# Hybrid decoder trunk on one core: pool halo copies, value-weight splits, the boundary norms and the MLP's token norm reordered

## The chip, the cores and the metric

The kernel runs on one core of one Trainium2 chip. TensorE (PE) multiplies matrices, VectorE (DVE), ScalarE (ACT) and GpSimd (POOL) work on elements, and SyncE (SP) issues most of the transfers. The metric is the device time of one execution in microseconds; a kernel's time is the median of its runs. The profiled execution is one more run, with its own time.

## What is computed

A decoder layer with a final norm, in float32, for one sequence of 2048 tokens of width 1024: a mixer (retention heads beside a causal pooling mixer) with an output projection, cross-attention into 256 memory tokens, and a gated MLP with a short convolution. The parts that the change touches:

```python
def rmsnorm(x, g):
    x32 = x.astype(jnp.float32)
    y = x32 * lax.rsqrt(jnp.mean(x32 * x32, axis=-1, keepdims=True) + EPS)
    return (y * g.astype(jnp.float32)).astype(x.dtype)

def pool_mixer(u, w, scale):
    ...
    for gi, wlen in enumerate(POOL_WINDOWS):      # 2, 4, 8, 16
        ...
        mean = (c - lower) / count                # mean over the trailing window
        groups.append(mean - u32[:, :, gi * POOL_GROUP:(gi + 1) * POOL_GROUP])
    ...

def cross_attn(h, mem_n, wq, wkv, wo):
    ...
    s = jnp.einsum('bshd,bmhd->bhsm', q, k).astype(jnp.float32) * (XA_HEAD_DIM ** -0.5)
    p = jax.nn.softmax(s, axis=-1).astype(v.dtype)
    o = jnp.einsum('bhsm,bmhd->bshd', p, v).reshape(B, S, D_MODEL)
    return o @ wo

def reference(...):
    ...
        x = x + jnp.concatenate([y_ret, y_pool], axis=-1) @ w_out[l]
        x = x + cross_attn(rmsnorm(x, xa_norm_g[l]), mem_n, xa_wq[l], xa_wkv[l], xa_wo[l])
        x = x + conv_glu_ffn(rmsnorm(x, ffn_norm_g[l]), ffn_w_up[l], ffn_conv_w[l],
                             ffn_conv_b[l], ffn_w_down[l])
    return rmsnorm(x, final_norm_g)
```

## The kernel before

**Arithmetic.** Each float32 operand is split in two rounded parts, high and low, and each product is three matmuls (high by high, high by low, low by high: L241, L242, L243 in `passes`). A split is two instructions: ACT copies the high part (L233), and DVE subtracts it from the original (L216, the line of the helper `tt`, which records most additions, subtractions and products). In the profile R is a raw weight as it came by DMA, Q a pair of its parts, G the arena that holds split activations and the diagonals, T a temporary, Z a larger buffer, mm a PSUM accumulator of a matmul, and aux a PSUM tile for small work.

**Stages.** Tokens go in two blocks of 1024, each as two halves of 512 columns; channels lie on the 128 partitions. For each block: the values, the four retention heads and four pool groups (`pool_group`), the output projection, the attention (`attention`), and its value products (`unit` with the weights `VWd`, eight tiles of 128 x 1024, each one of 48 matmuls). Then comes the MLP of both blocks (`run`). The memory-side weight products come first, beside block 0. All through block 0 and 1, `weight_sums` is stepped as `under[0]`: it adds MLP weight blocks in memory, by SP transfers and by accumulating POOL transfers (L919).

**What sets the order.** The program is written as Python generators that are stepped inside `unit` (one step of `behind[0]` after each quarter of a unit's matmuls). The framework then orders the instructions of each engine by a simulated timeline, inserts the semaphore waits, and leaves each engine a fixed sequence: what stands behind a waiting instruction on its engine waits too. `tc.issue_after(ins)` around a piece of code orders that piece's instructions behind `ins` where they are on the same engine.

**Pool group.** The evacuation `evac` (L627) takes the matmul result into u with 16 columns of room ahead, copies the previous half's last 16 columns in (L630) and saves this half's last 16 (L631), both on POOL; then DVE forms the window sums by doubling (1 to 4 additions of 128 x 527 to 128 x 513) and the result is split for the next product.

**Norms.** `stats` (L308) sums squared activations over partitions with one-column matmuls (L315) and runs three Newton steps on DVE; `rows_norm` (L1410) copies the result into rn. `spread` (L323) turns the 128 x 8 table into a row per token on all partitions: it splits rn (yh, yl), and for each half of 512 tokens DVE builds two diagonals (L216, G<-consts,yh and G<-consts,sm), PE multiplies them by ones (L339) and ACT copies the sum (L344). At the block boundary the generator `norms` (L1594) does this as `behind[0]`: the next block's table, the own block's table (used in the MLP), the spread. The four value weights of block 1 are loaded and split there too (L657), and pool groups 3 and 2 run ahead of the values.

**Attention.** 16 score tiles, eight for each of two pairs of heads. Each: matmuls, row maximum, exponential on ACT (L875), reciprocal and scaling on DVE; `turn` (L847) transposes the tile two tiles later (L850) and splits the result. The softmax scale comes from the norm of the block, formed after the first tile. The loads of the first VWd tiles go out during the attention, and their splits stand wherever the simulated timeline puts them. In block 1 the attention is stepped together with `first_tiles`, which forms the MLP's normed inputs of block 0 from tiles of Xd, and writes them and their sums to Hd.

**Token norm in the MLP.** For block 1 the normed inputs are formed during the MLP: `later_tiles` loads four half tiles of Xd and steps `normed_tiles` by a due-time list, one step every two ticks (`after(2, step)`); its first step does all four products.

Of the kernel before, what the change touches and what calls it, by code (L numbers as in the profile page):

```python
# [2 lines left out]

# [12 lines left out]
P = 128  # L16
# [5 lines left out]
SUB = 512  # L22
# [97 lines left out]
def trunk(ctx, tc, xT, memT, pos, w_qkgu, w_v, wkv, wqT, wo, wout_r, wout_p, poolT, w_up, w_dn, vecs, consts, outT):  # L120
# [156 lines left out]

    quarter, slow = [0], [True]
    behind, under, fetched = [iter(())], [iter(())], [None]

    def finish():
        for _ in behind[0]:
# [2 lines left out]
    def unit(raw, rhs, evac, order=range(4)):  # L285


        hs = pairs(raw)
        ps = [mmps() for _ in range(NS)]
        for h in range(2):  # L290
            for s in range(NS):
                for j, kk in enumerate(order):
                    k = 4 * h + kk
                    w = [hs[h][:, i, kk * P : (kk + 1) * P] for i in range(2)]
                    passes(ps[s], w, rhs(k, s), h + j == 0, h == 1 and j == 3)
                next(behind[0], None)
# [26 lines left out]
    def spread(y, outs, keep=True, late=False):  # L323

        yh = smp.tile([P, 8], F32R, tag="yh", name=nm("yh"), bufs=1)[:, : y.shape[1]]
        yl = small(y.shape[1])
        dve.tensor_copy(yh, y)
        tt(dve, yl, y, yh.bitcast(F32), ALU.subtract)
        at = 0

        one_pair = prs.take() if late else None
        for out in outs:
            n = out.shape[1] // P
            d = one_pair if late else B.take()
            ps = aux()[:, : n * P]
            for i, v in enumerate((yh.bitcast(F32), yl)):
                di = d.r[:, i * SUB : i * SUB + n * P]
                last = tt(dve, di.rearrange("p (a b) -> p a b", a=n), ident.rearrange("p (o b) -> p o b", o=1).to_broadcast([P, n, P]), bcast(v[:, at : at + n], P), ALU.mult)
                pe.matmul(ps, ones, di, start=i == 0, stop=i == 1)  # L339
# [6 lines left out]
        return last  # L346

    def squares(k, src, s_ap, eng=dve):

# [274 lines left out]
    def pool_group(b, g, rb):  # L624
        out = B.take(2)

        def evac(s, ps):  # L627
            u, *bufs = [TT.take() for _ in range(3 if g else 2)]
            tt(dve, u.f[:, 16 : 16 + SUB], ps, rb[s].f[:, :SUB], ALU.mult)
            pool.tensor_copy(u.f[:, 0:16], phalo[:, g])  # L630
            pool.tensor_copy(phalo[:, g], u.f[:, SUB : SUB + 16])  # L631
            src, lo = u, 1
            for i in range(g + 1):
                sh = 1 << i
                dst = bufs[i % 2]
                tt(dve, dst.f[:, lo : 16 + SUB], src.f[:, lo : 16 + SUB], src.f[:, lo - sh : 16 + SUB - sh], ALU.add)
                src = dst
                lo += 2 * sh
            cur, d = u.f[:, 16 : 16 + SUB], src.f[:, 16 : 16 + SUB]
            w = 2 << g  # L640
            if b == 0 and s == 0:
                tt(dve, d[:, :w], d[:, :w], icnt[:, :w], ALU.mult)
# [179 lines left out]
    def attention(sums, beside, pace):  # L822
# [24 lines left out]
        def turn(pt, t, e):  # L847
            tp = aux()
            for j in range(4):
                pe.transpose(tp[:, j * P : (j + 1) * P], e.f[:, j * P : (j + 1) * P], ident)  # L850
            pt4 = pt.r.rearrange("p (i k t) -> p i k t", i=2, t=T)[:, :, :, t * P : (t + 1) * P]
            split(tp.rearrange("p (k t) -> p k t", k=4), pt4[:, 0], pt4[:, 1])
            e.free()

        mw = [[], []]
        for _ in load_m(0):
            pass
# [568 lines left out]
    def normed_tiles(b, j, q, rb):  # L1426

        for i, v in enumerate(q):
            n, s = j + 4 * (i // 2), i % 2
            stt(v, v, ffng[:, n : n + 1], rb[s].f[:, :SUB], ALU.mult, ALU.mult)  # L1430
        if j == KT // 2 - 1:
            for r in rb:
                r.free()
        yield
        send(Hd[b, j], {0: q[0], 5: q[3], 3: q[2]})
        t = TT.take()
        todo = sums_of(*q, t.f[:, :SUB])
# [27 lines left out]
    def later_tiles(b, j, rb):  # L1465

        x = fetch_tiles(b, j)
        steps = normed_tiles(b, j, [r.f[:, :SUB] for r in x], rb)

        def step():  # L1470
            if next(steps, True) is None:
                after(2, step)
            else:
                for r in x:
                    r.free()

        after(2, step)
# [18 lines left out]
    for b in range(NB):  # L1496
# [68 lines left out]
        for n in range(KT):  # L1565
            if n + 1 < KT:
                fetch_acc(n + 1)

            def rhs(k, s):
                at = (k % 4) * T + s * SUB  # L1570
                return tuple(prob[k // 4].r[:, i * 4 * T + at : i * 4 * T + at + SUB] for i in range(2))

            unit(load_tile(VWd[n]), rhs, add_residual(b, n, xs, acc=acc[n]))
            act.dma_start(Xd[b, n], acc[n].f)
            if b + 1 < NB:
                load_x(n, nxt, got)
# [12 lines left out]
        if b + 1 < NB:  # L1589
            normed, own = [None, [], None], []  # L1590
            for u in acc:
                u.free()

            def norms(xs, nxt, normed, own):  # L1594

                normed[0] = rows_norm(nxt)
                yield
                own.append(rows_norm(xs))
                yield
                normed[1] += [TT.take() for _ in range(NS)]  # L1600
                spread(normed[0], [r.f[:, :SUB] for r in normed[1]])
                yield

            behind[0] = norms(xs, nxt, normed, own)
# [119 lines left out]
```

## Time and profile before

| | |
|---|---|
| runs | 2498.81, 2500.07, 2504.08 us; median 2500.07 |
| profiled execution | 2497.77 us, its span 2496.0 us |
| instructions in the span | 33121 |
| mean granted TensorE clock | 0.993 |
| moved by DMA | 474.27 MB, mean 190 GB/s |

The page divides the span into 40 slices of 62.4 us and prints tenths of busy time, and for the clock tenths of full speed:

```profile
PE   6999999999999999999998999999999999999997
DVE  8646566564636574665777776896677687877875
POOL 1010122100121110030025130332113021000001
PEclk9999999999999999999999999999999999999998
```

Slice 7 (374 to 437 us) holds the end of the last pool groups of block 0, slice 8 its first attention tiles, slice 10 (from 562) the beginning of its value products, slice 11 (624 to 686) the block boundary, slices 17 and 18 the attention of block 1, and from slice 20 on the MLP runs. A digit of 9 stands for 90% or more, so stalls of a few microseconds don't show in it: they are found in the waits, in short windows, and in the times at which matmuls start. A row of the timeline gives the start in us, the duration, engine, line, operation, output and inputs with their shapes, how many alike are merged (x2), and in brackets how long the engine had been idle before it and on what it waited.

### The profile page before, as it was taken

How to read it: one execution, taken by the hardware profiler on the slowest of the kernel's cores; microseconds unless marked ns; L12 is line 12 of the kernel's file. 1: busy time of each engine (PE TensorE's matmuls, PEld its weight loads, DVE VectorE, ACT ScalarE, POOL GpSimd, SP SyncE). 2: the span in 40 equal slices, each digit the busy share in tenths (PEclk: the TensorE clock that was granted, in tenths of full speed). 3: DMA queues.
4: the chain of work that ended last, by engine and by line, in shares of the span. 5: the costliest groups of instructions: out<-in, count | busy, mean ns of one | idle time of the engine just before them, and what ended most of it. 6: DMA issues, size and time to landing. Idle time of an engine off the chain costs nothing. (4 is left out here: it accounts for less than half of the span.)

```text
span 2496.0 us, 33121 instructions
## 1 busy us (share of the span) xinstructions
PE 2439.3 (98%) x11390; PEld 2035.1 (82%) x11390; DVE 1699.9 (68%) x2757; ACT 1220.0 (49%) x2171; POOL 387.9 (16%) x396
## 2 busy tenths in 40 slices
PE   6999999999999999999998999999999999999997
PEld 6888887888788888888886888888888887888885
DVE  8646566564636574665777776896677687877875
ACT  6333423443321223424654555675555576666663
POOL 1010122100121110030025130332113021000001
PEclk9999999999999999999999999999999999999998
DMA  9363888716766664365567565665456468768951
GB/s 319 90 169 110 249 189 233 234 41 207 218 142 151 155 158 153 108 226 210 174 205 251 179 195 161 202 228 171 158 164 210 136 217 297 245 190 281 343 165 68
DMA packets 257176, 474.27 MB, mean 190 GB/s; under 512 B 26864, under 2 KB 56176, under 8 KB 257008
## 3 DMA queue, kind: packets, MB, share of 16 engines
q1 hardware_dynamic: 212336, 408.18, 48.9%
q0 software_dynamic: 19584, 34.61, 9.0%
q10 hardware_dynamic: 25088, 29.37, 3.4%
q8 instruction: 89, 1.46, 0.2%
q14 instruction: 79, 0.65, 0.1%
HBM read 370.87 MB, written 170.39 MB: 217 GB/s over the span
## 5 line engine op out<-in xcount | busy, mean ns | idle before, releaser
L241 PE MATMUL mm<-G,Q 128*128 128x512 f32 (+1 forms) x1888 | 727.7, 386 | 18.9 <-ACT Q L233 10.9
L243 PE MATMUL mm<-G,Q 128*128 128x512 f32 (+1 forms) x1888 | 725.3, 385 | 4.6 <-DVE Q L216 4.5
L242 PE MATMUL mm<-G,Q 128*128 128x512 f32 (+1 forms) x1888 | 725.1, 384 | 0.0
L241 PE MATMUL mm<-G 128*128 128x512 f32 (+1 forms) x1380 | 530.0, 386 | 7.4 <-DVE Z L216 7.4
L243 PE MATMUL mm<-G 128*128 128x512 f32 (+1 forms) x1380 | 530.9, 385 | 2.3 <-DVE G L216 2.3
L242 PE MATMUL mm<-G 128*128 128x512 f32 (+1 forms) x1380 | 531.4, 385 | 0.0
L241 PEld LDWEIGHTS mm<-G,Q 128*128 128x128 f32 x1888 | 357.7, 190 | 88.1 <-ACT Q L233 11.5
L243 PEld LDWEIGHTS mm<-G,Q 128*128 128x128 f32 x1888 | 357.2, 189 | 74.4 <-DVE Q L216 5.9
L242 PEld LDWEIGHTS mm<-G,Q 128*128 128x128 f32 x1888 | 357.7, 189 | 68.4 <-DVE G L216 0.4
L241 PEld LDWEIGHTS mm<-G 128*128 128x128 f32 x1380 | 259.8, 188 | 61.0 <-DVE Z L216 7.3
L243 PEld LDWEIGHTS mm<-G 128*128 128x128 f32 x1380 | 259.8, 188 | 54.3 <-DVE G L216 2.8
L242 PEld LDWEIGHTS mm<-G 128*128 128x128 f32 x1380 | 259.9, 188 | 51.5
L225 DVE SCALAR_TENSOR_TENSOR Z<-Z,vecs 128x1024 f32<-128x1024 f32 x176 | 244.7, 1393 | 55.8 <-ACT Z L1067 50.2
L1004 ACT ACTIVATE G<-R 128x512 fp32r<-128x512 f32 (+1 forms) x272 | 167.1, 616 | 230.0 <-PE mm L242 223.7
L216 DVE TENSOR_TENSOR G<-R,G 128x512 fp32r<-128x512 f32 (+1 forms) x268 | 196.7, 741 | 115.4 <-ACT G L1004 76.8
L216 DVE TENSOR_TENSOR Q<-R,Q 128x512 fp32r<-128x512 f32 x235 | 174.0, 742 | 148.1 <-ACT Q L233 138.4
L216 DVE TENSOR_TENSOR Z<-Z,mm 128x512 f32<-128x512 f32 x284 | 193.3, 681 | 88.3 <-PE mm L243 87.8
L233 ACT ACTIVATE Q<-R 128x512 fp32r<-128x512 f32 x150 | 93.9, 627 | 238.5 <-PE mm L242 194.0
L216 DVE TENSOR_TENSOR G<-T,G 128x512 fp32r<-128x512 f32 (+1 forms) x201 | 134.8, 685 | 51.1 <-ACT G L953 37.7
L1004 ACT ACTIVATE Q<-R 128x512 fp32r<-128x512 f32 (+1 forms) x204 | 125.3, 614 | 76.4 <-PE mm L242 60.5
L1067 ACT ACTIVATE Z<-Z,vecs 128x1024 f32<-128x1024 f32 x88 | 109.3, 1242 | 51.6 <-DVE Z L216 50.0
L216 DVE TENSOR_TENSOR T<-T 128x512 f32<-128x512 f32 (+4 forms) x161 | 109.6, 689 | 35.1 <-POOL T L630 17.6
(217 smaller groups left out, 2654.9 us busy)
## 6 DMA issues: line engine op xcount, KB each, us to landing
R<-Ud SPq DMA_DIRECT2D x176, 256.0 KB, 2.7
T<-Gd SPq DMA_DIRECT2D x168, 256.0 KB, 4.3
R<-w_up SPq DMA_DIRECT2D x132, 256.0 KB, 3.0
Gd<-Z SPq DMA_DIRECT2D x110, 256.0 KB, 2.5
Ud<-w_up SPq DMA_DIRECT2D x88, 256.0 KB, 5.9
R<-w_qkgu SPq DMA_DIRECT2D x32, 512.0 KB, 4.3
R<-Dd SPq DMA_DIRECT2D x64, 256.0 KB, 4.1
Gd<-T SPq DMA_DIRECT2D x56, 256.0 KB, 3.1
```

Source lines behind the costliest of these rows:

```text
L216: return eng.tensor_tensor(out=out, in0=a, in1=b, op=op)
L225: dve.scalar_tensor_tensor(out=out, in0=a, scalar=s, in1=b, op0=op0, op1=op1)
L233: act.activation(hi, src, AF.Copy)
L241: pe.matmul(ps, lh, rh, start=start, stop=False, skip_group_check=more)
L242: pe.matmul(ps, lh, rl, start=False, stop=False, skip_group_check=more)
L243: pe.matmul(ps, ll, rh, start=False, stop=stop, skip_group_check=more)
L1004: act.activation(p2[:, 0, :w], self.raw[i].f[:, :w], AF.Copy)
L1067: act.activation(self.c[g].f, a[:, 2:], AF.Identity, bias=cb[:, f : f + 1], scale=cw[2][:, f : f + 1])
```

## The change

Four edits, here with the core of each.

*Pool group:* the two 16-column copies go to DVE.

```diff
-            pool.tensor_copy(u.f[:, 0:16], phalo[:, g])
-            pool.tensor_copy(phalo[:, g], u.f[:, SUB : SUB + 16])
+            dve.tensor_copy(u.f[:, 0:16], phalo[:, g])
+            dve.tensor_copy(phalo[:, g], u.f[:, SUB : SUB + 16])
```

On DVE, in the last pool groups of block 0 (aux, mm and T with a number are single tiles; phalo holds the 16 columns):

```order
 L216 TENSOR_TENSOR T<-mm_2973,T 128x512
 L216 TENSOR_TENSOR Q<-R,Q 128x512
+L654 COPY T<-phalo 128x16
 L225 TENSOR_SCALAR T<-aux_2925,vecs,T 128x512
 L216 TENSOR_TENSOR T<-mm_2972,T 128x512
+L655 COPY phalo<-T 128x16
 L216 TENSOR_TENSOR T<-T 128x527
 L216 TENSOR_TENSOR G<-T,G 128x512
+L654 COPY T<-phalo 128x16
```

The copies that a window sum (128x527) needs now stand ahead of it in DVE's own sequence.

*Value weights:* every turn notes its ACT copy in `turned`, and the splits of the first two VWd tiles are ordered on ACT behind the eleventh; `unit` takes pairs that are already split.

```diff
-        hs = pairs(raw)
+        hs = raw if isinstance(raw, list) else pairs(raw)
...
-            split(tp.rearrange("p (k t) -> p k t", k=4), pt4[:, 0], pt4[:, 1])
+            turned.append(act.activation(pt4[:, 0], tp.rearrange("p (k t) -> p k t", k=4), AF.Copy))
+            tt(dve, pt4[:, 1], tp.rearrange("p (k t) -> p k t", k=4), pt4[:, 0].bitcast(F32), ALU.subtract)
...
-            unit(load_tile(VWd[n]), rhs, add_residual(b, n, xs, acc=acc[n]))
+            with tc.issue_after(turned[10].ins) if n < 2 else nullcontext():
+                weights = pairs(load_tile(VWd[n]))
+            unit(weights, rhs, add_residual(b, n, xs, acc=acc[n]))
```

On DVE in the first attention, before: one such split (Q<-R) among the steps on the norm's 128x8 table.

```order
L225 TENSOR_SCALAR sm_3791<-sm_3791,sm_3788 128x8
L216 TENSOR_TENSOR Q<-R,Q 128x512
L225 TENSOR_SCALAR sm_3789<-sm_3791,sm_3789 128x8
L216 TENSOR_TENSOR sm_3791<-sm_3789 128x8
L225 TENSOR_SCALAR sm_3791<-sm_3791,sm_3788 128x8
```

Now, later in the same attention: three of them behind the low part of a turned tile (G<-aux).

```order
L220 TENSOR_SCALAR sm_4338<-sm_4338,scl_3731 128x2
L216 TENSOR_TENSOR G<-aux_4347,G 128x4x128
L216 TENSOR_TENSOR Q<-R,Q 128x512 x3
L903 RECIPROCAL sm_4339<-sm_4339 128x2
L220 TENSOR_SCALAR T<-T,sm_4339 128x256 x2
```

The split has left the table's steps; ACT's three copies moved the same way, and in the second attention the three splits stand behind the same turn. Its sixth VWd load is issued on SP later than before, behind some loads of Xd tiles and stores to Hd.

*Block boundary:* the spread comes in two steps, all four diagonals and then all four matmuls, and the own block's table comes last.

```diff
+    def spread_steps(y, outs):
+        ...
+        dve.tensor_copy(yh, y)
+        tt(dve, yl, y, yh.bitcast(F32), ALU.subtract)
+        ...
+        for at in range(0, len(outs) * n, n):
+            d = B.take()
+            ds.append(d)
+            for i, v in enumerate((yh.bitcast(F32), yl)):
+                ...
+                tt(dve, di.rearrange("p (a b) -> p a b", a=n), ident.rearrange("p (o b) -> p o b", o=1).to_broadcast([P, n, P]), bcast(v[:, at : at + n], P), ALU.mult)
+        yield
+        for d, out in zip(ds, outs):
+            ps = aux()
+            for i in range(2):
+                pe.matmul(ps, ones, d.r[:, i * SUB : (i + 1) * SUB], start=i == 0, stop=i == 1)
+            d.free()
+            act.activation(out, ps, AF.Copy)
+        yield
...
                 normed[0] = rows_norm(nxt)
                 yield
+                normed[1] += [TT.take() for _ in range(NS)]
+                todo = spread_steps(normed[0], [r.f[:, :SUB] for r in normed[1]])
+                next(todo)
+                yield
+                next(todo)
+                yield
                 own.append(rows_norm(xs))
-                yield
-                normed[1] += [TT.take() for _ in range(NS)]
-                spread(normed[0], [r.f[:, :SUB] for r in normed[1]])
                 yield
```

On PE at the boundary, before: the first two ones-matmuls (128x512) with weight matmuls between.

```order
L243 MATMUL mm_5099<-G,Q 128x512
L339 MATMUL aux_5197<-G,ones 128x512
L241 MATMUL mm_5099<-G,Q 128x512
L242 MATMUL mm_5099<-G,Q 128x512
L243 MATMUL mm_5099<-G,Q 128x512
L339 MATMUL aux_5203<-G,ones 128x512
```

Now: the four together, with the own block's column sums (128x1) among them.

```order
L243 MATMUL mm_5099<-G,Q 128x512
L316 MATMUL aux_5207<-consts,T 128x1
L367 MATMUL aux_5176<-G,ones 128x512
L316 MATMUL aux_5207<-consts,T 128x1
L367 MATMUL aux_5180<-G,ones 128x512
L316 MATMUL aux_5207<-consts,T 128x1 x2
L367 MATMUL aux_5176<-G,ones 128x512
L316 MATMUL aux_5207<-consts,T 128x1
L367 MATMUL aux_5180<-G,ones 128x512
L316 MATMUL aux_5207<-consts,T 128x1 x3
```

The next block's sums are followed by 36 weight matmuls at a stretch, then comes this group. On DVE the own table's Newton steps, which stood between the two halves of the diagonals, now come behind all of them, among the first window sums.

*Token norm:* for block 1 the generator stops after each of the first three products, and a step is due every tick.

```diff
             stt(v, v, ffng[:, n : n + 1], rb[s].f[:, :SUB], ALU.mult, ALU.mult)
+            if b and i < 3:
+                yield
...
-                after(2, step)
+                after(1, step)
```

In the MLP the sequences of DVE, ACT and POOL are the same as before; on SP one load of an Xd tile stands a place or two earlier, near the beginning of the MLP.

More of the change, by code (lines that the diff above doesn't have):

```diff
@@ L1 @@
 import math
-from contextlib import ExitStack
+from contextlib import ExitStack, nullcontext
 import concourse.bass as bass
@@ L279, in trunk @@
     behind, under, fetched = [iter(())], [iter(())], [None]
+    turned = []
     def finish():
@@ L346, in spread @@
         return last
+    def spread_steps(y, outs):
+        yh = smp.tile([P, 8], F32R, tag="yh", name=nm("yh"), bufs=1)[:, : y.shape[1]]
+        yl = small(y.shape[1])
+        dve.tensor_copy(yh, y)
+        tt(dve, yl, y, yh.bitcast(F32), ALU.subtract)
+        n = SUB // P
+        ds = []
+        for at in range(0, len(outs) * n, n):
+            d = B.take()
+            ds.append(d)
+            for i, v in enumerate((yh.bitcast(F32), yl)):
+                di = d.r[:, i * SUB : (i + 1) * SUB]
+                tt(dve, di.rearrange("p (a b) -> p a b", a=n), ident.rearrange("p (o b) -> p o b", o=1).to_broadcast([P, n, P]), bcast(v[:, at : at + n], P), ALU.mult)
[7 more added lines that the diff above has]
+        yield
     def squares(k, src, s_ap, eng=dve):
@@ L851, in turn @@
             pt4 = pt.r.rearrange("p (i k t) -> p i k t", i=2, t=T)[:, :, :, t * P : (t + 1) * P]
-            split(tp.rearrange("p (k t) -> p k t", k=4), pt4[:, 0], pt4[:, 1])
+            turned.append(act.activation(pt4[:, 0], tp.rearrange("p (k t) -> p k t", k=4), AF.Copy))
+            tt(dve, pt4[:, 1], tp.rearrange("p (k t) -> p k t", k=4), pt4[:, 0].bitcast(F32), ALU.subtract)
             e.free()
+        turned.clear()
         mw = [[], []]
```

## The prediction

> **What bounds the kernel now.** I began with busy time by engine, went on to what TensorE waits for, and then to the stretches in which the change works.
>
> ```profile
> PE 2439.3 (98%) x11390; PEld 2035.1 (82%) x11390; DVE 1699.9 (68%) x2757; ACT 1220.0 (49%) x2171; POOL 387.9 (16%) x396
> PE mm L243 <- DVE G L216: 2.3, 1, 2.3
> PE aux L850 <- DVE T L220: 1.6, 3, 0.9
> 350.00:450.00 100.00, 97.89 (x442) 81.03 (x441) 61.32 (x115) 29.04 (x56) 21.37 (x32) 0.98 0.80 212
> 650.00:750.00 100.00, 97.45 (x438) 80.67 (x437) 49.10 (x99) 25.74 (x43) 24.91 (x31) 0.98 0.69 181
> 1350.00:1450.00 100.00, 92.85 (x397) 75.76 (x396) 76.53 (x82) 53.32 (x79) 29.10 (x24) 0.97 0.60 200
> ```
>
> The first row says that TensorE (PE) is busy for 2439.3 of 2496.0 us. The waits are microseconds in all, how often, and the longest. The last three rows are stretches of 100 us: busy time of PE, weight loads, DVE, ACT, POOL, the granted clock, DMA share, GB/s. No edit removes a matmul, so an edit can gain only what PE stands still, or runs at a lower granted clock, in its own stretch. That is about 2 us in each of the first two stretches and 7 in the third, plus the clock's 2 to 3% there. Everything below is therefore a hunt for single stalls. I go by start-to-start distances of matmuls, since modelled ends overlap.
>
> **The change part by part.** *Halo copies from POOL to DVE.* Four pool groups, two blocks and two halves with two copies each make 32 moved instructions.
>
> ```profile
> 381.74 0.81 POOL L919 DMA_DIRECT2D Ud<-Ud  x1 [4.59 <-DMA Ud<-w_up]
> 382.27 0.48 POOL L630 COPY T<-phalo 128x16 f32<-128x16 f32 x1
> 382.79 0.71 DVE L216 TENSOR_TENSOR T<-T 128x527 f32<-128x527 f32 x1 [8.02 <-POOL T L630]
> 387.55 0.39 PE L242 MATMUL mm<-G,Q 128*128 128x512 f32 x1
> 387.78 0.39 PE L243 MATMUL mm<-G,Q 128*128 128x512 f32 x1
> 390.28 1.22 PE L241 MATMUL mm<-G,Q 128*128 128x512 f32 x2 [2.11 <-ACT G L233]
> 391.30 0.63 PE L242 MATMUL mm<-G,Q 128*128 128x512 f32 x1
> 391.73 0.63 PE L243 MATMUL mm<-G,Q 128*128 128x512 f32 x1
> 390.20:393.61 3.41, 3.33 (x8) 2.62 (x9) 3.41 (x6) 1.14 (x3) 1.07 (x2) 0.50 1.03 378
> 687.52 1.32 DVE L216 TENSOR_TENSOR T<-T 128x527 f32<-128x527 f32 x2 [6.16 <-POOL T L630]
> L1412 DVE COPY rn<-sm 128x8 f32<-128x8 f32 x5 | 0.9, 176 | 0.2
> ```
>
> In the first block POOL stood 4.59 us in a memory-to-memory weight addition (L919) that waited for its operand; the copy of L630 was queued behind it, and DVE waited 8.02 us for that copy before the window sums. The sums came late, so the split that feeds the next matmul came late, and PE stood. The distance 387.78 to 390.28 is 2.50 us, where the pair before shows 387.78 - 387.55 = 0.23: 2.27 us lost. Then the granted clock is 0.50 for one window of 3.41 us, in which matmuls start every 391.73 - 391.30 = 0.43 us: eight of them at 0.20 too much, and about 0.2 more at the first, make 1.77. On DVE the copy waits for no one. A 16-column DVE copy is not in the trace; the nearest row is an 8-column one at 176 ns. Eight copies of 0.18 cost DVE 1.4 us in this stage, against 8.02 removed, so the stall should go whole: **-4.05 us**. Bounds: 0, if something else holds DVE as long, to -4.05. At the three other such waits (the longest, 6.16 us at 687.52) PE has no gap: nothing to win. In the second block the same 1.4 us of DVE are covered by these waits; without that cover they would cost at most 1.4.
>
> *Value-weight splits behind a turned tile, first attention.*
>
> ```profile
> 489.13 0.63 ACT L233 ACTIVATE Q<-R 128x512 fp32r<-128x512 f32 x1 [7.68 <-DMA R<-VWd]
> 489.80 0.69 DVE L216 TENSOR_TENSOR Q<-R,Q 128x512 fp32r<-128x512 f32 x1 [4.44 <-ACT Q L233]
> 495.76 0.70 PE L850 MATMUL aux<-consts,T 128*128 128x128 f32 x4 [0.87 <-DVE T L220]
> ```
>
> ACT waited 7.68 us for a weight that nobody needed before 575, and DVE's half of that split stood inside the Newton steps of the attention's norm, 4.44 us. The softmax scale came late by that, and the first transposes waited 0.87 us; start to start the gap is 1.04 us over the usual. With the splits behind the eleventh turn this goes: **-1.04 us**, bounds 0 to -1.04 (the Newton steps may be late for another reason). Behind the split on ACT stands the exponential's table load, which comes earlier as well.
>
> *The same in the second attention.* There the splits ran spread over turns; now three pairs stand in a row on ACT and DVE behind the eleventh turn, and the next reciprocal and softmax scaling are queued behind them.
>
> ```profile
> 1094.42 0.68 DVE L216 TENSOR_TENSOR G<-aux,G 128x512 fp32r<-128x512 f32 x1
> 1095.92 0.17 DVE L877 RECIPROCAL sm<-sm 128x2 f32<-128x2 f32 x1 [0.82 <-ACT T L875]
> 1099.53 0.75 DVE L225 SCALAR_TENSOR_TENSOR T<-T,vecs 128x512 f32<-128x512 f32 x1 [1.28 <-DMA T<-Xd]
> 1352.35 1.78 DVE L216 TENSOR_TENSOR Q<-R,Q 128x512 fp32r<-128x512 f32 x1
> ```
>
> Three splits of 0.68 us (the duration of the first row, same shape) are 2.05 us, and DVE's idle time right there is 0.82 + 1.28 = 2.10: **0 us**. Bounds: at 1.78 us each, as beside POOL's additions in the fourth row, they take 5.34, so 3.2 more than the cover; on the other side the splits leave the stretch before, and the short stalls of this attention could go, -1.2 (the 1.6 of the L850 wait in all less what the first attention holds, and a little spacing). I take zero, since 0.68 is what all DVE rows of this stage show. By the Trainium skill, "SBUF — State Buffer", section "Who interferes with whom", a DVE instruction with two SBUF inputs contends with a GpSimd instruction that reads SBUF, and the loser is fully blocked. These splits have two such inputs and POOL adds tiles here, so by the rule alone this term would be nearer +3.2; the 1.78 us row agrees with the rule, the 0.68 rows show that it seldom strikes in this stage. One weight load is also issued on SP behind tile loads instead of ahead of them; it is wanted some 50 us later, so it costs nothing itself.
>
> *The norms at the block boundary.* Before, PE did the next block's column sums, 12 matmuls, the own block's column sums, 15 matmuls, and then the four ones-matmuls with 13 others between. Now 36 matmuls come first, and the ones-matmuls and the own sums form one group at the end, with nothing between.
>
> ```profile
> 663.26 0.54 SPq L657 DMA_DIRECT2D R<-w_v  x1
> 663.21 0.73 PE L241 MATMUL mm<-G,Q 128*128 128x512 f32 x1
> 667.64 1.84 PE L315 MATMUL aux<-consts,T 128*128 128x1 f32 x16
> 669.57 1.15 ACT L233 ACTIVATE G<-R 128x512 fp32r<-128x512 f32 x2 [2.46 <-DMA R<-w_v]
> 671.44 0.16 DVE L222 TENSOR_SCALAR sm<-aux 128x8 f32<-128x8 f32 x1
> 674.06 1.29 DVE L216 TENSOR_TENSOR G<-consts,yh 128x512 fp32r<-128x512 f32 x2
> 676.55 1.28 DVE L216 TENSOR_TENSOR G<-consts,sm 128x512 fp32r<-128x512 f32 x2
> 674.89 0.47 PE L339 MATMUL aux<-G,ones 128*128 128x512 f32 x1 [1.85 <-DVE G L216]
> 678.90 0.40 PE L242 MATMUL mm<-G,Q 128*128 128x512 f32 x1
> DMA to landing us min/median/max: 3.7/4.6/9.1
> 659.86:663.27 3.41, 2.71 (x22) 2.47 (x20) 3.41 (x6) 3.41 (x8) 0.53 (x1) 1.00 0.35 98
> 663.27:666.69 3.42, 3.42 (x9) 2.68 (x9) 3.42 (x7) 1.67 (x4) 0.22 (x1) 0.50 0.93 301
> 1356.18:1359.59 3.41, 1.68 (x7) 1.24 (x7) 3.41 (x3) 0.00 (x0) 3.33 (x3) 1.00 0.79 270
> 1359.59:1363.00 3.41, 0.21 (x1) 0.00 (x0) 3.18 (x4) 2.29 (x4) 3.33 (x3) 1.00 0.91 333
> ```
>
> The diagonals are late because DVE's norm steps (from 671.44) stand behind the split of a value weight, for which ACT waited 2.46 us on its DMA. The diff leaves that order as it was. So the first diagonal stays at about 674.1, and with the own norm out of the way the last two start near 676.1 instead of 676.55 and end by 677.4. PE: the 12 matmuls reach 667.64 as before; 24 more at 0.23 reach 673.1; the four ones-matmuls and eight column sums then follow the diagonals and end about 678.4 (677.4, a spacing of 0.23, three sums at about 0.2 each). At 678.90 the old order had the same done and 40 matmuls, so it is four ahead: 678.4 + 4 x 0.23 - 678.9 = **+0.4 us**. The old stall of 1.85 us does not vanish; it is longer, and the own sums (some 1.7 us) fill part of it.
>
> Between 673.1 and 678.4 PE has then only four wide matmuls. The rows at 659.86 and 663.27 show what came of a thin stretch: a window of 22 entries, mostly one-column sums, and behind it one at clock 0.50. The two last rows show the opposite: 1.68 us busy with wide matmuls, and the next window still at 1.00. The stretch in question is nearer to the first, its wide matmuls fewer. I count one such window, 3.41 us at half speed: 1.7 us lost, **+1.7 us**, bounds 0 to 3.4 for none or two. By the Trainium skill, "TensorE: Matmul & The Clock Gate", section "What's actually happening", the clock falls to half after at least one idle window of 3413 ns. The length of 3.41 agrees; that a window must be idle throughout does not, since the window ahead of 663.27 was 2.71 us busy. By that rule the term would be 0 and the sum 1.7 us lower.
>
> *The MLP's token norm, one tile a step.*
>
> ```profile
> 1346.66 0.75 DVE L225 SCALAR_TENSOR_TENSOR T<-T,vecs 128x512 f32<-128x512 f32 x1 [5.23 <-DMA T<-Xd]
> 1350.48 0.75 DVE L225 SCALAR_TENSOR_TENSOR T<-T,vecs 128x512 f32<-128x512 f32 x1 [2.48 <-DMA T<-Xd]
> ```
>
> This is what a finer step could cure: norm products stand ahead of MLP work on DVE and wait for their tile, and PE pays for it: 2.3 us at 1355 (the G row of the waits), and in the whole stretch from 1350 to 1450 7.1 us not busy and 3% of the clock, some 10. But DVE's, ACT's and POOL's instructions in the MLP come out in the same order as before; only one tile load on SP goes a place or two earlier, near 1240. **0 us**; bounds 0 to -8, most of those 10, should the earlier load change the phase.
>
> The sum: -4.05 - 1.04 + 0 + 0.4 + 1.7 + 0 = -3.0. The profiled execution took 2497.77 us, span 2496.0; the median of the runs is 2500.07, 2.3 above it. So 2494.8 on the profiled execution and **2497 us** on the median.
>
> **The rivals.** *No slow window, chance 0.25.* If PE's activity in 673 to 678 suffices, or the value weight lands 1 to 2 us sooner and the diagonals with it, the boundary costs nothing: -5.1 to -7, so 2493 to 2495. For it: the window at 1356.18, half busy, with full clock behind it; against it: 663.27. *The boundary loses, chance 0.15.* The ones group hangs on one weight load with no matmuls between to cover it. Issue to landing of these loads is 3.7 to 9.1 us, by the landing row; the last took about 6.3, from its issue at 663.26 until ACT began at 669.57. At 9.1 PE stands 3 us longer, and a second slow window adds 1.7: -3.0 + 4.7 = +1.7, 2502; with contended splits in the second attention up to 2505. It decides from 3 us of extra lateness. Against it: the median of 4.6. *The copies do not free DVE, chance 0.12.* If DVE is itself behind at 382, the stall of 2.50 us stays: -1.04 + 2.1 = +1.1, 2501. Against it: 8.02 us of pure waiting. *The MLP shifts after all, chance 0.06*: -3 - 8, 2489.
>
> **How the numbers follow.** The forecast has 0.42, with its own range 2495 to 2500. What a measurement of this kernel can tell from no change is about 0.2%, 5 us. Faster by more needs 2495 or less: nearly all of the MLP case, two thirds of the first rival, a few hundredths of the forecast, 0.27. Slower by more needs 2505: a part of the second rival, and reorderings elsewhere that I have not priced, 0.14. The rest, 0.59, is within. The range 2491 to 2504 leaves out the MLP case and the far part of the second rival, and allows for medians that differ by 1 or 2 us.
>
> **What would show it.** Right: no DVE wait for a copy near 382 and matmuls 0.23 us apart through 387 to 394 at clock 1.00; no DVE wait at 490; the transposes of the first attention on time; at the boundary one group of ones-matmuls with a gap of about 2 us ahead and a window at 0.50 behind; in the MLP the same stall some 4 us earlier. Wrong: a stall that stays at 388, a gap in PE near 1100 to 1115, or slow windows in the MLP that come or go, which would outweigh all of these.

## The result and the profile after

The changed kernel takes 2496.18 us (median of 21 runs) where the kernel before takes 2501.07 (21 runs): ratio 0.9984, 95% interval 0.9976 to 0.9991, so 2 to 6 us faster. The profiled execution has a span of 2493.6 us against 2496.0. The forecast was 2497 us and a change within 0.2%.

First the busy row, the waits of PE and the three stretches of the page before, now of the changed kernel (columns as there).

```profile
PE 2440.1 (98%) x11390; PEld 2037.7 (82%) x11390; DVE 1703.1 (68%) x2789; ACT 1219.0 (49%) x2171; POOL 372.5 (15%) x364
PE aux L367 <- DVE G L216: 1.6, 2, 1.2
PE mm L243 <- DVE G L216: 1.2, 1, 1.2
350.00:450.00 100.00, 100.00 (x459) 83.33 (x458) 65.09 (x132) 30.44 (x57) 16.25 (x20) 1.00 0.83 218
650.00:750.00 100.00, 97.39 (x423) 80.82 (x422) 46.64 (x104) 25.03 (x41) 18.90 (x23) 0.95 0.70 180
1350.00:1450.00 100.00, 93.99 (x407) 77.02 (x406) 77.65 (x85) 53.07 (x79) 28.48 (x24) 0.98 0.63 203
```

In the first stretch PE is now busy throughout at full clock (97.89 and 0.98 before). In the second it is as busy as before, but the granted clock fell from 0.98 to 0.95. The third is a little better, with no engine's order changed there; the experiments show how much of that is chance.

Stalls of this size are lost when one page is compared with another. But all kernels here issue the same 10464 weight matmuls in nearly the same order, so the time between two of them that have the same numbers can be compared directly. Worked out from the starts of all matmuls, in us against the profiled execution of before; the columns are places on the clock of before, and the last is all together; the rest of it lies in the first 200 us and in 505 to 650, and everywhere else the kernels agree within 0.1 (e7_ownfirst, which computes something else, is left out):

```
                200-  372-  480-  650-  1050-  1320-  1620-  2050-  all
                300   405   505   690   1125   1375   1660   2125
changed        +2.0  -4.0  -1.1  +3.4   -0.7   -1.7   +1.1   -1.5  -2.4
e1_halo        +3.3  -4.0  -1.1  +1.4   -1.2   -1.3   +0.5   -0.9  -2.9
e2_splits      +3.3  +2.6  -1.1  +0.3   -1.1   -0.4   +0.4   -0.8  +4.6
e3_bound       +0.8  -0.9  -1.1  +2.8   +0.1   -0.9   +0.1   +1.5  +2.9
e4_token       +0.7  -0.2  -0.7   0.0   +0.4   -0.6   +0.8   +0.9  +2.7
e5_nobound     +1.9  -4.0  -1.0  +0.6   -1.1   -1.7   +1.2   +0.4  -1.0
e6_ownlast     +1.8  -4.0  -1.1  +0.6   -0.9   -1.7    0.0   -0.5  -4.5
e8_wv          +1.9  -4.0  -1.1  -3.3   -1.1   -1.1   +1.5   -1.3  -7.5
e9_filled      +0.1  -4.0  -1.1  +5.0   -0.9   -0.7   +0.4   -0.5  -0.2
e10_wv_again   +2.1  -4.0  -1.1  +0.8    0.0   +0.1   +0.2   +0.3  +1.9
e11_after_ag.  +4.4  -4.0  -1.1  +2.4   -0.8   +0.4   +0.7   -0.9  +3.0
e12_wv_both    +3.2  -4.0  -1.1  -4.5   -0.5   -1.5   -0.1   -0.2  -8.5
```

The first row is the change: -4.0 at the pool groups, -1.1 at the first attention, +3.4 at the block boundary, -0.7 at the second attention (1050 to 1125), and four places where nothing was edited, or nothing that PE saw. One execution of each is in the table, so a single entry may be chance; a column that splits the kernels by an edit with no overlap is hard to put down to it. How far executions differ is told by e4_token, whose engines run the same sequences as before's, and by e8_wv and e10_wv_again, which are one and the same program: they have -3.3 and +0.8 at the boundary.

**The pool groups.** DVE, then PE, and one window of the granted clock, of the changed kernel:

```profile
375.31 0.17 DVE L654 COPY T<-phalo 128x16 f32<-128x16 f32 x1 [1.31 <-PE aux L801]
377.02 0.17 DVE L655 COPY phalo<-T 128x16 f32<-128x16 f32 x1
377.11 0.70 DVE L216 TENSOR_TENSOR T<-T 128x527 f32<-128x527 f32 x1
389.77 0.39 PE L243 MATMUL mm<-G,Q 128*128 128x512 f32 x1
390.00 0.62 PE L241 MATMUL mm<-G,Q 128*128 128x512 f32 x2
389.92:393.33 3.41, 3.41 (x17) 2.83 (x16) 3.41 (x9) 0.69 (x2) 2.52 (x3) 1.00 0.38 50
```

A copy takes 0.17 us, the window sum starts at 377.1 where it started at 382.8, and the matmul for which PE stood 2.50 us now follows 0.23 us after the one before, at clock 1.00.

**The boundary.** ACT, DVE, PE and the clock's windows of the changed kernel:

```profile
666.67 1.15 ACT L233 ACTIVATE G<-R 128x512 fp32r<-128x512 f32 x2 [2.17 <-DMA R<-w_v]
668.54 0.16 DVE L222 TENSOR_SCALAR sm<-aux 128x8 f32<-128x8 f32 x1
671.24 1.29 DVE L216 TENSOR_TENSOR G<-consts,yh 128x512 fp32r<-128x512 f32 x2
673.04 1.29 DVE L216 TENSOR_TENSOR G<-consts,sm 128x512 fp32r<-128x512 f32 x2
670.49 0.28 PE L316 MATMUL aux<-consts,T 128*128 128x1 f32 x2
671.98 0.50 PE L367 MATMUL aux<-G,ones 128*128 128x512 f32 x1 [1.21 <-DVE G L216]
674.46 0.78 PE L367 MATMUL aux<-G,ones 128*128 128x512 f32 x1
675.03 1.27 PE L316 MATMUL aux<-consts,T 128*128 128x1 f32 x6
676.17 0.77 PE L241 MATMUL mm<-G,Q 128*128 128x512 f32 x1
676.74 0.63 PE L242 MATMUL mm<-G,Q 128*128 128x512 f32 x1
670.64:674.05 3.41, 1.83 (x12) 1.50 (x11) 3.31 (x9) 0.00 (x0) 0.81 (x1) 1.00 1.05 312
674.05:677.46 3.41, 3.41 (x13) 3.02 (x13) 2.09 (x6) 1.19 (x2) 1.31 (x2) 0.50 1.07 381
677.46:680.88 3.42, 3.42 (x9) 2.65 (x9) 3.26 (x11) 0.00 (x0) 0.99 (x2) 0.50 1.07 320
```

The order of events is the forecast one: the value weight's DMA is waited for, the norm steps follow it, PE runs its 36 matmuls and stands, and the group comes as the diagonals do. But behind it stand two windows at half clock, not one. PE is counted busy for the whole first of them, yet mostly with one-column sums: four wide matmuls, that is with 512 columns, start in it (674.46, 676.17, 676.74, 677.17). One more slow window, at 660.4, lies ahead of all this; it is the one that the kernel before has at 663.27.

### The profile page after: what moved, and what is told of

Same layout as the page of the kernel before. It is cut to its first block, busy times and chain, and to the rows that moved or that the text cites. A ratio compares the mean times of both kernels' runs of the same rounds, so it can differ in the third digit from the quotient of the medians.

```text
span 2493.6 us, 33068 instructions
## 1 busy us (share of the span) xinstructions
PE 2440.1 (98%) x11390; PEld 2037.7 (82%) x11390; DVE 1703.1 (68%) x2789; ACT 1219.0 (49%) x2171; POOL 372.5 (15%) x364
## 5 line engine op out<-in xcount | busy, mean ns | idle before, releaser
L964 ACT ACTIVATE aux<-R 128x512 f32<-128x512 f32 (+1 forms) x184 | 105.4, 575 | 51.1 <-DVE Q L216 27.9
```

Source lines behind the costliest of these rows:

```text
L964: act.activation(t, x, AF.Copy)
```

## The experiments

**Each edit alone.** Each kernel is the one before with one of the four edits of the diff, unchanged:

```diff
e1_halo    pool.tensor_copy -> dve.tensor_copy, twice
e2_splits  + with tc.issue_after(turned[10].ins) if n < 2 else nullcontext():
e3_bound   + todo = spread_steps(...), own.append(rows_norm(xs)) last
e4_token   + yield per tile; after(2, step) -> after(1, step)
```

> Only the pool group's two copies go from POOL to DVE; all else as before. Theory: the whole gain at 388 to 394 us comes from this, -4.0 us (ratio about 0.9984), with matmuls 0.23 us apart there and no slow window, and nothing is given back at the block boundary. Rival: the copies, now on DVE among the first window sums of block 1, are what made the boundary slower in the changed kernel (+3.4 us there); then this kernel shows -0.6 us (0.9998) and two slow windows near 675 us.

Measured: ratio 0.9975 (0.9965 to 0.9985). At 372 to 405 us the profile shows -4.0, the window sum at once after the copies:

```profile
378.55 0.18 DVE L631 COPY phalo<-T 128x16 f32<-128x16 f32 x1
378.63 0.70 DVE L216 TENSOR_TENSOR T<-T 128x527 f32<-128x527 f32 x1
```

The boundary is 1.4 us longer in this execution, with one slow window as before, not two: the rival falls. By its ratio this one edit gives the whole gain of the change or more, though the two intervals overlap. All seven kernels of the table with copies on DVE besides the changed one and e1 show -4.0 in this column; the three with copies on POOL show +2.6, -0.9 and -0.2, so the stall there comes in every execution, and in one it was 2.6 us worse. The slow window behind it does not: before and e2 have one or two, e3 and e4 have a second gap of PE of some 0.9 us in its place.

> Only the value-weight splits are ordered behind the eleventh turn. Theory: -1.0 us at the first attention's transposes (496 us) and -0.7 us at the end of the second attention (1110 to 1115 us), together -1.7 us, ratio about 0.9993. Rival: the second attention's -0.7 is chance, and the splits under POOL's additions cost as much as they save: -1.0 us or less, and DVE splits near 1095 us that take over 1 us each.

Measured: 0.9993 (0.9984 to 1.0002), which is no clear difference. In the table it has -1.1 at 480 to 505 and -1.1 at 1050 to 1125. But e1 and e3, without this edit, have -1.1 at the first place too, and e1 at the second. So the stall of before's profile at 496 was one draw: among the four kernels without the edit it was 1.04 us, 0.4, and twice nothing. With the edit it is nothing in every execution. At the second attention the kernels with the edit have +0.6 to -1.1, with a mean of -0.7 over ten (e7_ownfirst, below, has the +0.6), those without 0, -1.2, +0.1 and +0.4. The means differ by about half a microsecond at each place, but at the second the two groups overlap, so a gain there is not shown. The rival's long splits are there, three in 4.00 us from 1100.34 on, and PE loses nothing by them that the table shows.

> Only the norms at the block boundary are changed (diagonals a step ahead, own table last). Theory: this edit alone loses 3.4 us between 660 and 682 us (ratio about 1.0014): PE reaches the group of ones-matmuls about 2 us before the first diagonal, and the thin stretch is followed by two windows at half clock. The prediction's term was +2.1 us (1.0008). Rival: the loss needs the halo copies on DVE as well; then this kernel is the same as before within 1 us.

Measured: 1.0005 (0.9994 to 1.0016), so the time alone does not decide. The profile does: +2.8 us at 650 to 690, and PE's rows show the mechanism in full without any halo copy on DVE:

```profile
670.25 0.39 PE L243 MATMUL mm<-G,Q 128*128 128x512 f32 x1
674.07 0.50 PE L366 MATMUL aux<-G,ones 128*128 128x512 f32 x1 [2.84 <-DVE G L216]
677.36 1.27 PE L315 MATMUL aux<-consts,T 128*128 128x1 f32 x6
674.75:678.16 3.41, 3.41 (x14) 3.13 (x14) 2.36 (x4) 1.16 (x2) 1.50 (x3) 0.50 1.05 389
678.16:681.58 3.42, 3.42 (x10) 2.79 (x10) 2.19 (x6) 0.04 (x1) 0.65 (x1) 0.50 1.09 304
```

PE stands 2.84 us, and the granted clock is at half for 6.8 us from 674.7 on. The three kernels of the table with this edit as it is (changed, e3, e11) have +2.4 to +3.4 and two slow windows behind the group; the four without (e1, e2, e4, e5) 0.0 to +1.4, and never more than one slow window in the whole stage. The rival falls. The early slow window near 660 is missing in e3 and e11; there PE comes to the group sooner and stands 2.84 us where the changed kernel stands 1.21, so the wait for the diagonals takes up what the early window costs.

> Only the token norm steps one tile at a time, one step a tick. Theory: no engine's sequence changes, so the time is that of before (1.0000, within 0.0008), and its profile shows what one execution differs from another by: the stalls near 276, 1355 to 1370, 1637 and 2070 to 2115 us come out 1 to 2 us longer or shorter without any change. Rival: the token norm is behind the 1.7 us that the changed kernel saves at 1355 to 1370 us; then 0.9993 or less, and one slow window there instead of two.

Measured: 0.9998 (0.9988 to 1.0007). Its profile measures chance: with every engine's sequence as before, the places of the MLP come out at -0.6, +0.8 and +0.9, and the sum at +2.7. It still has two slow windows at 1364, and the POOL copy's stall, here with the wait of 8.20 us where before had 8.02:

```profile
384.00 0.81 POOL L919 DMA_DIRECT2D Ud<-Ud  x1 [4.15 <-PE mm L242]
385.05 0.71 DVE L216 TENSOR_TENSOR T<-T 128x527 f32<-128x527 f32 x1 [8.20 <-POOL T L630]
392.57 0.73 PE L241 MATMUL mm<-G,Q 128*128 128x512 f32 x2 [2.32 <-ACT G L233]
```

**The boundary, taken apart.** All of these keep the halo copies on DVE and the splits behind the turn.

```diff
e5_nobound   the boundary as before
e6_ownlast   next table; spread between matmuls as before; own table last
e7_ownfirst  next table; own table; then spread_steps in two steps
```

> The changed kernel with the block boundary as before (next table, own table, spread between matmuls). Theory: the boundary edit costs the changed kernel its 3.4 us, so this one shows 0 to +1.4 us there and -4.0 at 372 to 405 us; ratio 0.9970 to 0.9978 to before, below the changed kernel's 0.9984. Rival: the two slow windows at the boundary come from the stage standing 4 us earlier in a fixed grid of windows, whatever the order there; then they are here too, with 0.9984.

Measured: 0.9977 (0.9967 to 0.9987), and +0.6 at the boundary, with the one slow window. That is where the theory put it, though the interval overlaps the changed kernel's; the profile, not the time, shows that the boundary's loss goes with the boundary's edit.

> The changed kernel with the own table last as in the change, but the ones-matmuls spread among weight matmuls as before. PE now has 24 weight matmuls and seven column sums ahead of the first ones-matmul instead of 36. Theory: it is the missing matmuls between the ones-matmuls that make the thin stretch; here 3, 5 or 6 stand between, so the stall ahead of the first is longer by about 0.7 us than before, but there is at most one slow window: +0.5 to +2 us at 650 to 690 us against before. Rival: own table last is the cause, by the column sums that now fill the stall at a poor rate; then +3 us or more with two slow windows, as in the change.

Measured: 0.9988 (0.9978 to 0.9997), +0.6 at 650 to 690, but with two slow windows, from 669.2 on. Neither side: the loss is the theory's, the windows are the rival's. A likely reason, though not tested alone, is that here the last value weight was asked for early: its load was issued 0.7 us ahead of the first column sums, in the changed kernel 2.9 us behind them. So the diagonals began at 668.9, some 3 us sooner after these sums, and that gain can have hidden the loss. The window ahead of the slow ones is again full of one-column sums, and no wide matmul starts in it:

```profile
666.38 1.72 PE L316 MATMUL aux<-consts,T 128*128 128x1 f32 x14 [0.32 <-DVE sm L222]
665.75:669.16 3.41, 2.04 (x16) 1.64 (x14) 2.97 (x16) 0.21 (x1) 0.00 (x0) 1.00 1.06 336
669.16:672.58 3.42, 2.97 (x8) 2.49 (x9) 3.32 (x10) 0.00 (x0) 0.81 (x1) 0.50 1.06 337
```

> The changed kernel with the own table ahead of the spread again, but all four diagonals still a step ahead of the ones-matmuls. PE has 12 matmuls, the own sums and then 24 matmuls ahead of the first ones-matmul, and reaches it at about 674.9 on the clock of before, when the first diagonal is ready. Theory: no stall of PE there and no second slow window: -2.0 us at 650 to 690 us against before, -5 against the changed kernel; ratio to before 0.9965 to 0.9972. Rival: the own table's Newton steps on DVE push the last two diagonals back, and the group of ones-matmuls waits for them as long as before: 0 us.

This kernel computes something else at one place: the first half of pool group 3 is scaled with its row before the row is written. Its time, 0.9979 (0.9970 to 0.9988), is therefore only a hint: 0.0 at the boundary, no second slow window, but stalls of 0.1 and 0.6 us inside the group, since the last two diagonals wait for the own table's steps. The gain of 2 us did not come; the rival is nearer.

> The changed kernel with twelve more 128x512 matmuls of ones by block inputs ahead of the ones-matmuls, whose result is overwritten (the output is unchanged). They stand behind 24 weight matmuls, and the own sums now come last of all. Theory: what brings a slow window is a window of 3.41 us with fewer than six 512-column matmuls; filled like this, every window has more, so no slow window follows the boundary, and the loss there against before is +2.2 us (PE reaches the first ones-matmul with three matmuls and all own sums undone), less than the change's +3.4 although PE does 2.7 us of work for nothing. Rival: a stall of about 1.8 us brings the slow window by its idle time, whatever the matmuls around it: +3.9 us with one or two slow windows between 670 and 685 us.

```diff
         for d, out in zip(ds, outs):
             ps = aux()
+            for k in range(6):
+                pe.matmul(ps, ones, X[:, k, :SUB], start=True, stop=True)
             for i in range(2):
```

Measured: 0.9991 (0.9981 to 1.0000), +5.0 at the boundary. A miss. The fillers went out at 664.7, as soon as they could, and PE stood behind them:

```profile
664.67 2.97 PE L367 MATMUL aux<-G,ones 128*128 128x512 f32 x12
672.05 0.80 PE L369 MATMUL aux<-G,ones 128*128 128x512 f32 x1 [4.18 <-DVE G L216]
666.41:669.82 3.41, 1.47 (x7) 0.84 (x5) 2.21 (x9) 1.67 (x3) 0.00 (x0) 1.00 1.06 332
669.82:673.23 3.41, 1.18 (x3) 0.99 (x4) 3.17 (x12) 0.00 (x0) 0.81 (x1) 0.50 1.07 326
```

So the premise failed: the stretch was not filled, five wide matmuls start in the window ahead of the slow one. It fits the count that was proposed, but was not the test that it was meant to be; what a truly filled stall would do was not tried.

**What holds the diagonals.** If they are late for the value weight's DMA, moving that wait away must remove the stall. These kernels have the boundary's order of before, and e8 and e10 are the same program.

```diff
e8_wv, e10_wv_again
-                spread(normed[0], [r.f[:, :SUB] for r in normed[1]])
+                normed[2] = spread(normed[0], [r.f[:, :SUB] for r in normed[1]])
...
-            wv = [value_weights(kp) for kp in range(KT // 2)]
+            with tc.issue_after(last.ins):
+                wv = [value_weights(kp) for kp in range(KT // 2)]
e12_wv_both (copied[0] is ACT's copy of the spread row)
+            with tc.issue_after(last.ins), tc.issue_after(copied[0].ins):
```

> Halo copies and splits as in the change, the boundary as before, but DVE's halves of the four value-weight splits of block 1 are ordered behind the last diagonal. Theory: the diagonals are late only because the norm steps stand behind a split that waits for its weight's DMA; here they come 2 to 3 us earlier, so PE's stall of 2.0 us goes: -2 us at 650 to 690 us, ratio about 0.9968. Rival: the column sums of the next block, not the split, hold the norm steps, and the eight splits in a row delay the first window sums: 0 to +2 us.

Measured: 0.9973 (0.9961 to 0.9985), -3.3 at the boundary, and no slow window:

```profile
650.00:750.00 100.00, 98.88 (x453) 82.28 (x452) 50.38 (x109) 25.77 (x42) 19.82 (x24) 1.00 0.72 186
658.50 0.38 SPq L658 DMA_DIRECT2D R<-w_v  x1
669.59 0.33 SPq L306 DMA_DIRECT2D R<-w_qkgu  x1
```

> Halo copies, splits, and value-weight splits behind the last diagonal, a second time, beside the changed kernel on the same chip. Theory: about 0.9970 to before again, and 3 to 5 us under the changed kernel, with no stall ahead of the ones-matmuls and no slow window between 655 and 690 us. Rival: the first time was a lucky execution; then the same as the changed kernel within 1.5 us.

Measured: 0.9970 (0.9958 to 0.9982), a median of 2493.67 us beside 2497.54 of e11_after_again, which runs the changed kernel's sequences: 3.9 us under it, though their intervals against before overlap. But this execution shows +0.8 at the boundary, with two slow windows from 668.3 on, so the second half of the expectation missed. The profile shows the rest of the wait: only DVE's halves had been moved.

```profile
665.98 0.63 ACT L233 ACTIVATE G<-R 128x512 fp32r<-128x512 f32 x1 [2.13 <-DMA R<-w_v]
667.68 0.69 DVE L216 TENSOR_TENSOR Q<-R,Q 128x512 fp32r<-128x512 f32 x1 [2.50 <-ACT Q L233]
669.03 1.87 PE L316 MATMUL aux<-consts,T 128*128 128x1 f32 x8 [2.31 <-DVE T L216]
```

ACT waits 2.13 us for w_v, behind it stand a split and a square, and so the own column sums are late and PE waits 2.31 us for them. In e8's execution ACT waited 2.00 us there and PE 1.12, and no slow window followed: the same order can come out either way.

> The changed kernel without the token norm's finer steps: every engine's sequence is that of the changed kernel. Theory: 0.9984 to before again, with two slow windows at 670 to 685 us. Rival: the finer steps matter after all; then the time leaves the changed kernel's interval of 0.9976 to 0.9991.

This is the changed kernel without the last edit of the diff. Measured: 0.9982 (0.9972 to 0.9991), two slow windows from 676.6 on. The finer token norm does nothing that can be measured, and the change repeats.

> Halo copies and splits as in the change, the boundary's order as before, and now both halves of the four value-weight splits behind the spread: ACT's behind its copy of the spread rows, DVE's behind the last diagonal. Theory: in the kernel with DVE's halves alone moved, ACT still stood in the value weight's DMA with the next split and a square for the own sums behind it, so the column sums were late by 1.4 to 2.6 us; with both moved nothing at the boundary waits for that DMA: -3 us or more at 650 to 690 us against before, no slow window there, ratio 0.9965 to 0.9972. Rival: the four raw buffers are then held some 10 us longer, the next head's weights come late, and PE stands after 690 us: no better than DVE's halves alone (0.9970 to 0.9973), or worse.

Measured: 0.9966 (0.9953 to 0.9978), 2489.76 us beside 2497.97. ACT's eight halves now run in one go behind the spread, the norm steps wait for nothing, and PE does not stop (ACT, DVE, PE, then the stretch of 100 us):

```profile
673.68 4.27 ACT L233 ACTIVATE G<-R 128x512 fp32r<-128x512 f32 x8
664.07 0.16 DVE L222 TENSOR_SCALAR sm<-aux 128x8 f32<-128x8 f32 x1
666.69 1.29 DVE L216 TENSOR_TENSOR G<-consts,yh 128x512 fp32r<-128x512 f32 x2
668.80 0.39 PE L341 MATMUL aux<-G,ones 128*128 128x512 f32 x1
650.00:750.00 100.00, 100.00 (x458) 83.26 (x457) 53.27 (x112) 27.26 (x44) 19.85 (x24) 1.00 0.74 190
```

In 650 to 750 us PE is busy for 100.00 at clock 1.00, where before had 97.45 and 0.98: -4.5 us at the boundary. The raw buffers that are held longer cost nothing that PE shows. By its ratio this is the best of the kernels run, some 8 us under the one before, but its interval overlaps those of e8 and e10, and against the changed kernel it was not timed on the same chip.

One rival is left open. With the splits moved, the loads that SP issues next come later too: in e8 the next head's weights (w_qkgu) are issued 11 us behind the last value weight, where before had one 2.3 us ahead of it and one 1.4 us behind, with weight sums' transfers between. The last value weight then takes 3.6 to 3.7 us from issue to landing in e8, e10 and e12, and 6.0 to 7.6 in the eleven other profiles. In e12 the norm steps wait for no split, so its gain does not hang on that; in e8 and e10, where ACT still waits for the weight, how much comes from the order and how much from the faster load is not shown.

## Why the prediction was right

The time, its sign and its place in the range held, and the terms' mechanisms with them, but several sizes were off. That the sum came out near is in part luck: by the times the halo copies give more than forecast, and the boundary loses more and the first attention gives less.

- **Halo copies, -4.05.** Measured -4.0 in every profile with the copies on DVE. The cover named for the second block held as well: 690 to 1050 us differs by 0.0. (Four other waits for these copies are in the profile of before, not three; none had a gap of PE.) That the stall was typical was taken for granted: the four profiles with the copies on POOL differ by up to 3.5 us there, and only two of them have the slow window that was priced at 1.77. By the times the edit alone gives 0.9975, some 6 us, with an interval from 3.8 to 8.8.
- **First attention, -1.04.** The profile has -1.1, but e1 and e3 have it without the edit. The term was read from one unlucky execution: about -0.4 on average. What failed is the step from one profile's stall to the kernel's.
- **Second attention, 0.** On average -0.5, which is within the scatter. The 0.68 us taken for each split was wrong: the three took 4.01 us, between the two bounds of 2.05 and 5.34. Two of them, beside two additions of POOL, took 1.70 and 1.78, and the third, begun behind these, 0.68; two long ones and a short one are in all ten kernels with the edit.

```profile
1093.71 4.01 DVE L216 TENSOR_TENSOR Q<-R,Q 128x512 fp32r<-128x512 f32 x3
1093.57 3.00 POOL L216 TENSOR_TENSOR T<-T 128x512 f32<-128x512 f32 x2 [0.40 <-DMA Hd<-T]
```

So the splits outran the cover of 2.10, and yet PE lost nothing there. The cover was mis-stated: DVE's idle time at that spot is not the slack of the turn, which PE takes two tiles later. That the term came out near zero is luck.

- **Boundary, +0.4 of lateness and +1.7 of clock.** The sum was +2.1, measured +3.4, +2.8 and +2.4 in three executions. The diagonals came as worked out (first pair within 0.1 us, last pair 0.6 us earlier, relative to the first column sums). Mis-sized is the clock: one slow window was counted behind the group, and two came each time, since the first one again has few wide matmuls, and column sums in their place. Until the last diagonal is done, PE would stand in any case: that takes 0.3 us of the first slow window in the changed kernel, 1.7 in e3 and 1.3 in e11. Half of what is left of the two windows is 3.3, 2.6 and 2.8 us, an estimate that leaves +0.1, +0.2 and -0.4 for the lateness. The bound of 3.4 covered it. The Trainium skill's rule, weighed at that place ("TensorE: Matmul & The Clock Gate", "What's actually happening"), would have given 0; that the window ahead must be idle does not hold here: 1.83 us of busy PE preceded the slow windows.
- **MLP, 0.** Right: -2.1 in the changed kernel's profile over the three places, +0.2 in its twin e11, +1.1 in e4. This is the spread of executions, as is the +2.0 at 200 to 300 us, ahead of the first edited instruction: there ACT waits for a store of VWd to free its buffer, 3.92 us before and 7.85 in the changed kernel.

Of the rivals, the boundary that loses came nearest: it did lose 1.3 us more than the forecast, by its second slow window, though not by a late weight, which took 6.0 us from issue to landing, 6.3 before. The 9.1 us in that rival's price is a misreading: the landing row mixes the loads of both blocks, and 9.1 is one of the first block's, issued at 47.7 us. Still, the diagonals do wait for this load while a split stands ahead of the norm steps: in e12, where none does, they came 7.7 us behind the first column sums, in the changed kernel 13.5.

## What to carry to other kernels

Work that the array will wait for should not be queued behind an instruction that waits for a transfer: a copy of 0.5 us on POOL cost 4 us because of the weight addition ahead of it, and a weight split on ACT and DVE did the same to a norm. Before gathering small matmuls into a group, see how many wide ones remain in the window around it. And where the stall that an edit should remove hangs on a DMA, take a second profile of the same kernel before sizing it: here two executions of the same order differed by 1 us at the first attention and by 4 us at the boundary.

## What the runs showed of the hardware

The granted clock is set in windows of 3.41 us on a fixed grid, and what tells beforehand whether a window will be slow is not PE's busy time but how many wide matmuls start in the window ahead of it. I counted 128x512 matmuls (a narrower one by its columns) in every window at full clock from 100 to 2460 us of the fourteen profiles, and noted the clock of the window behind it:

```
wide matmuls in the window     0 to 4     5     6     7 or 8
next window at half clock        26       5     4        0
next window at full clock         0       1    10       63
```

With seven or more the next window was never slow, with four or fewer always. Busy time does not part them: windows ahead of a slow one were busy for 0 to 3.28 us, and one ahead of a full one for only 1.50. At most 15 fit in a window at 0.23 us, so somewhat under half of the possible was enough. A window at half clock ends by the same count: with up to six it was followed by another slow one in 17 of 19 cases, with seven or eight, the full number at 0.43 us, by a full one in 33 of 34. One-column sums keep PE busy in the profile (2.71 us in the window ahead of 663.27, 3.41 in the one from 674.05) and count for almost nothing. This is read off the profiles, and no run set the count on purpose; whether columns, rows or switching activity is what is measured stays open.
